# Gate projections as seven half-size products in a hybrid decoder layer on one core

## The chip, the cores and the metric

One core of one Trainium2 chip runs the whole program. The metric is device time in microseconds from launch to end. Before the change, three runs took 2067.43, 2071.05 and 2077.85 us, median 2071.05. A further execution was recorded by the hardware profiler; it took 2070.41 us, and its page and trace are what is read here.

## The reference

One layer of a decoder, 4096 tokens of width 1024, float32:

```python
h = _rmsnorm(x, g_pre) * (1.0 + scale[:, None]) + shift[:, None]
proj = h @ w_in
aq, ak, av, ag, rkv, rg, gq, gkk, gv, gg = jnp.split(proj, ...)
attn = _sliding_window_attention(...) * jax.nn.silu(ag)
rwkv = _rwkv7_mixer(h, ...) * jax.nn.silu(rg)
gla = _gla_mixer(h, gq, gkk, gv, ...) * jax.nn.silu(gg)
y = jnp.concatenate([attn, rwkv, gla], axis=-1) @ w_out
return x + gate[:, None] * _rmsnorm(y, g_post)
```

The gates `ag` (512 columns), `rg` and `gg` (256 each) are together one product of h (4096 x 1024) with a 1024 x 1024 weight. The change is about this product. The output product `@ w_out` has the same size.

## The kernel before

**Numbers.** Each float32 operand of a projection is split into a float16 high part and a float16 rest, and a product is three matmuls, high x high, high x rest and rest x high, added up in PSUM. Weights are scaled by a power of two before the split; the scale comes from the sum of their squares.

**Two phases.** Tokens go in 16 tiles of 256 (`NS = 16`, `NT = 256`). Phase one makes h of each tile (`stage_a`, kept in `hscr` as two float16 parts), and runs RWKV and GLA, whose results go to `mscr`. Beside it, `stage_c` prepares weights for phase two in small pieces: it reads a piece (tile `cs`), squares and sums it on ScalarE, splits it (ScalarE and VectorE, tile `ch`) and writes it to `wscr` (seven sets of 256 columns: two of q, one of k and v, four of gates) or, for the output product, to `woscr`. Phase two, from about 1000 us on, does per tile: q, k, v projections (`qkv`, `heads_of`; PSUM tiles `qp`, `kp`, `vp`), the gates (`gates`, `gates_of`; PSUM tile `gp`), the sliding-window attention (`stage_s`, `attend`; scores `sc`, values `ovp`), the mixing of heads and gates (`stage_m`), and the output product with its norm (`outp`, `norm`; PSUM tile `op`).

**The gates before.** `gates_of` makes four quarters of 256 channels. Each is 2 x 8 x 3 matmuls with weights as the stationary operand and 256 tokens of h as the moving one; ScalarE's tanh and one VectorE instruction per quarter make z (1 + tanh) of the PSUM bank in `ag`. All four weight quarters stay in SBUF. There are two `ag` buffers, used in turn.

**The output product** already has the form that the gates get: seven products of half size (Strassen's scheme in Winograd's form), whose weight sums are made in phase one (`wo_group`) and whose activation sums are made by VectorE in `stage_m`. Four of the seven weight sets stay in SBUF, three are streamed from `woscr` into one buffer `Wv`, half a set (512 KB) at a time. The activation blocks are split into `mtp`, four buffers in turn (`block`), scaled by `msc`; `msc` comes from the squares of the mixed tile, which a matmul with ones adds up over partitions (PSUM tile `mp`, then `mtot` and the small steps of `pow2` on VectorE). So the first block of a tile waits for all its gates.

**What sets the order.** The program is written as generators (`streams`, `emit`), and in each phase every instruction goes through `Order.note`, which gives it a rank: its place in the program, less `URGENT` for instructions that are marked urgent (PSUM drains). `Order.pin` then plays the program through with a table of costs and fixes the order of each engine's queue, lowest rank first among what is ready. The queues are worked in that order. The table of costs knows nothing of waits between VectorE and GpSimd. PSUM has two banks for projections and products (`pj`), so a product can start only when the one before the last has been drained.

In phase two, `stage_p2(i)` writes for most tiles: `gates(i)` after `outp(i - 1)`, then `qkv(i + 1)`. All instructions are issued through one helper line, so the profile shows them under L334 and they are told apart by their tiles.

## Time and profile before

| what | value |
|---|---|
| median of three runs | 2071.05 us |
| the profiled execution | 2070.41 us |
| its span, first to last instruction | 2068.6 us |
| mean granted TensorE clock | 0.986 |
| busy: TensorE, VectorE, ScalarE, GpSimd | 94%, 78%, 56%, 10% of the span |
| moved by DMA | 241.99 MB, mean 117 GB/s |
| chain that ended last, by engine | PE 57%, DVE 24%, DMA 8%, ACT 6% |

The span leaves 1.8 us of the execution outside it. PE is TensorE's matmuls, PEld its weight loads, DVE VectorE, ACT ScalarE, POOL GpSimd, SP the queue that issues DMAs. Matmuls are pipelined: one of 256 columns is listed with 273 ns but the next starts about 109 ns after it, so rates are read from start times. Neighbouring VectorE instructions overlap by some 0.08 us in the listing. In a group's row, the numbers behind the bar are busy time and mean ns of one instruction, then the idle time before them and what ended it.

### The profile page before, as it was taken

Reading aid. Unit: us, or ns where it says so; the run is one execution under the profiler, and the core shown is the slowest. Engines: PE = TensorE matmul, PEld = TensorE weight load, DVE = VectorE, ACT = ScalarE, POOL = GpSimd, SP = SyncE. Lnnn points to the kernel's source line nnn. Section 1 sums busy time; section 2 is a strip of 40 time slices with the busy share of each in tenths; the row PEclk is TensorE's granted clock in tenths of the full one; section 3 lists DMA queues with packets and bytes.
Section 4 is the critical chain, followed back from the end, with each engine's and each line's share of the span. In section 5 each row is a group of like instructions: output and inputs, shape, how many; then the busy total and the mean of one; then the engine's idle time right before and its main releaser. Section 6 shows DMA issues by size and latency. Waiting matters only on the chain.

```text
span 2068.6 us, 61564 instructions
## 1 busy us (share of the span) xinstructions
PE 1954.1 (94%) x24931; PEld 1516.6 (73%) x24931; DVE 1610.2 (78%) x5211; ACT 1154.7 (56%) x2765; POOL 216.6 (10%) x405
## 2 busy tenths in 40 slices
PE   5899999999999999999888999999999999999997
PEld 2677777787877877777667677777877777877783
DVE  5777878878777788987767878877778877778877
ACT  5867676677766856766334444453444444444543
POOL 0510111421111111111100000000000000000000
PEclk8999999999999999999999999999999999999999
DMA  9332232334222412446314534333334333334314
GB/s 344 126 95 80 74 97 72 108 104 120 81 93 68 138 45 92 119 122 177 117 43 151 166 113 146 105 134 107 123 116 142 109 126 115 114 125 128 123 45 175
DMA packets 183898, 241.99 MB, mean 117 GB/s; under 512 B 52195, under 2 KB 141748, under 8 KB 179382
## 3 DMA queue, kind: packets, MB, share of 16 engines
q1 hardware_dynamic: 183462, 237.45, 35.5%
q8 instruction: 198, 3.24, 0.7%
q14 instruction: 94, 0.77, 0.1%
q10 hardware_dynamic: 144, 0.52, 0.1%
HBM read 177.08 MB, written 60.82 MB: 115 GB/s over the span
## 4 chain that ended last, share of the span: by engine, by line
PE 57%; DVE 24%; DMA 8%; ACT 6%; issue 3%; SPq 2%; DVEq 0%; POOL 0%; ACTq 0%; POOLq 0%
PE gp L334 16%; PE op L334 12%; PE zz L334 5%; PE qp L334 3%; PE lp L334 3%; PE sc L334 2%; SPq L334 2%; DVE mtp L334 2%; DVE q L334 2%; PE ovp L334 2%; PE kp L334 2%; DVE pr L334 2%; PE pv L334 2%; DMA cs<-in_wo 1%; DMA cs<-in_w 1%
## 5 line engine op out<-in xcount | busy, mean ns | idle before, releaser
L334 PEld LDWEIGHTS <-mtp 128*128 128x128 f16 x1344 | 130.3, 98 | 140.9 <-issue 3.5
L334 PE MATMUL op<-o,mtp 128*128 128x512 f16 x768 | 172.3, 379 | 0.1
L334 ACT ACTIVATE pr<-pr,nm,lsc 128x256 f32<-128x256 f32 (+1 forms) x256 | 149.3, 585 | 33.7 <-DVE nm L334 33.7
L334 PE MATMUL op<-ov,mtp 128*128 128x512 f16 x576 | 143.1, 379 | 0.3 <-DVE q L334 0.2
L334 PEld LDWEIGHTS <-hT 128*128 128x128 f16 x1536 | 117.1, 99 | 25.8 <-DVE kg L334 4.3
L334 DVE CUSTOM_DVE_ANT_0 pr<-sc,ab,sinks 128x256 f32<-128x256 f32 (+1 forms) x256 | 108.6, 476 | 11.4 <-PE sc L334 11.1
L334 DVE TENSOR_TENSOR yv<-op,yv 128x512 f32<-128x512 f32 x105 | 70.4, 681 | 47.8 <-PE op L334 33.7
L334 PE MATMUL pv<-gvh,hT 128*128 128x272 f16 x512 | 100.1, 286 | 6.2 <-DVE kg L334 3.1
L334 ACT ACTIVATE ag<-gp,gh 128x512 f32<-128x512 f32 x64 | 43.7, 683 | 109.4 <-PE gp L334 109.4
L334 POOL COPY kT<-kT 128x512 f16<-128x512 f16 x15 | 10.2, 677 | 845.2 <-DVE kT L334 816.0
L334 ACT ACTIVATE mtp<-yv,oi 128x1024 f16<-128x1024 f32 x30 | 34.3, 1143 | 111.7 <-DVE yv L334 111.2
L334 PE MATMUL lp<-hT,Lh 128*128 128x256 f16 x512 | 92.4, 274 | 0.1
L334 PE MATMUL zz<-hT,rh 128*128 128x256 f16 x512 | 90.4, 276 | 0.0
L334 PE MATMUL zz<-hT,vh 128*128 128x256 f16 x512 | 88.8, 273 | 1.4 <-DVE zb L334 1.4
L334 DVE SCALAR_TENSOR_TENSOR ag<-ag,gp 128x512 f32<-128x512 f32 x64 | 43.8, 684 | 59.6 <-ACT ag L334 59.5
L334 PE MATMUL zz<-hT,kh 128*128 128x256 f16 x512 | 89.8, 273 | 0.0
L334 PE MATMUL gqk<-hT,gqkh 128*128 128x256 f16 x512 | 89.4, 275 | 0.0
L334 PE MATMUL gp<-hT,q3h 128*128 128x256 f16 x512 | 86.9, 274 | 1.9 <-DVE yv L334 1.4
L334 PE MATMUL gp<-hT,q5h 128*128 128x256 f16 x512 | 87.0, 273 | 1.4 <-DVE ag L334 1.4
L334 PE MATMUL qp<-hT,q1h 128*128 128x256 f16 x512 | 85.8, 273 | 0.6 <-DVE kT L334 0.6
L334 PE MATMUL qp<-hT,q0h 128*128 128x256 f16 x512 | 85.2, 273 | 1.1 <-DVE nwt L334 1.1
L334 PE MATMUL gp<-hT,q6h 128*128 128x256 f16 x512 | 85.5, 273 | 0.0
(460 smaller groups left out, 6046.0 us busy)
## 6 DMA issues: line engine op xcount, KB each, us to landing
ov<-woscr SPq DMA_DIRECT2D x96, 512.0 KB, 3.9
xt<-in_x SPq DMA_DIRECT2D x16, 1024.0 KB, 5.3
hscr<-hT SPq DMA_DIRECT2D x16, 1024.0 KB, 5.3
hT<-hscr SPq DMA_DIRECT2D x16, 1024.0 KB, 5.1
x<-in_x SPq DMA_DIRECT2D x30, 512.0 KB, 4.3
out<-yv SPq DMA_DIRECT2D x30, 512.0 KB, 2.9
cs<-in_w SPq DMA_DIRECT2D x112, 128.0 KB, 2.4
v<-vscr SPq DMA_DIRECT2D x128, 64.0 KB, 2.5
```

The source lines that it names most:

```text
L334: r = f(*args, **kw)
```

## The change

Seven products of half size replace the gates' eight half-size quarters of work (two halves of the channels x two halves of the contraction x two halves of the tokens):

- Weights. Phase one makes the seven weight sums of the gates (`group` with `gate` set, pieces of 512 columns) and keeps them in `gwscr`; the output product's sums go through the same function, in 8 groups instead of 16. `wscr` keeps only the three sets of q, k and v. The two column halves of the gates can have different scales, so the right half is first brought to the left half's (`g_r`).
- Activations. `sums`, per tile, makes four sums of quarters of h on GpSimd: four additions that join the high part and the rest, four additions and differences, and for each of the four sums a ScalarE copy to float16 and a GpSimd difference for the rest: 12 GpSimd instructions on 512 columns. Scratch tiles X, Y, Z are `xg`, the results `sg`.
- Products. `gates_of` runs seven products with a 128-column moving operand. ScalarE copies products 0 and 4 to X, VectorE adds the others to what is there already, GpSimd does two additions more (`g12`, and `Z`), and `close` makes z (1 + tanh) from SBUF with X, Y, Z as scratch.
- Streaming. Four of the gates' sets stay, three are streamed into `Wv`, which the output product uses too; `feed` issues the next half in the order in which the two products come (`runs`). The last tiles get buffers of their own (`ENDS`).
- Order. k and v are projected ahead of the gates and q after them (`mid`); the sums of the next tile are written behind q. One `ag` buffer is left. `URGENT` is 600 instead of 150, and block splits and `mix_scale` are marked urgent too.

```diff
-URGENT = 150
+URGENT = 600
...
+        def group(gate, k, c):
+
+            src, base, sc = (w2, 3, g_sc[c]) if gate else (wo, 0, wo_sc)
+            left, right = [wt([P, 512], "cs", 2).rearrange("p (h n) -> p h n", h=2) for _ in range(2)]
...
-            if 4 <= i < 6:
-                yield from wo_squares(i - 4)
-            elif 6 <= i < NS - 2:
-                for g in (i - 6, i + 2):
-                    yield from wo_group(g % 4, g // 4)
+            if 3 <= i < 5:
+                for n in (i, i + 2):
+                    yield from gate_squares(n)
+            elif 5 <= i < 7:
+                yield from wo_squares(i - 5)
+            for _ in range((0, 0, 0, 0, 1, 1, 1, 2, 2, 2, 2, 2, 2, 1, 0, 0)[i]):
+                yield from group(*next(groups))
...
+    PRODUCTS = ((0, False), (1, True), (6, True), (3, False), (4, True), (5, True), (2, False))
+    GATES = ((0, False), (6, True), (1, True), (4, False), (3, True), (5, True), (2, False))
...
+        def whole(t, i, j):
+            G.tensor_tensor(t, quarter(hT, 0, i, j), quarter(hT, 1, i, j), op=ALU.add)
+
+        def parts(t, n):
+            S.copy(to[n][:, 0], t)
+            G.tensor_tensor(to[n][:, 1], t, to[n][:, 0], op=ALU.subtract)
+
+        whole(X, 1, 0)
+        whole(Y, 1, 1)
+        G.tensor_tensor(Y, X, Y, op=ALU.add)
+        parts(Y, 0)
+        whole(Z, 0, 0)
+        G.tensor_tensor(Y, Y, Z, op=ALU.subtract)
+        parts(Y, 1)
+        G.tensor_tensor(X, Z, X, op=ALU.subtract)
+        parts(X, 2)
+        whole(Z, 0, 1)
+        G.tensor_tensor(Z, Z, Y, op=ALU.subtract)
+        parts(Z, 3)
...
-        for n in range(4):
-            yield ["pj"]
-            gp_ = pj("gp")
-            for b in range(2):
-                yield from proj(gp_[:, b * NT : (b + 1) * NT], Wq[3 + n], b * P, P, hT)
-            av = ag[:, 2 * n : 2 * n + 2, :].rearrange("p b n -> p (b n)")
-            model.order.urgent = URGENT
-            S.activation(av, gp_, AF.Tanh, scale=g_h[n])
-            V.scalar_tensor_tensor(av, av, 1.0, gp_, op0=ALU.add, op1=ALU.mult)
-            model.order.urgent = 0
+        moving = (a11, s2, a12, s3, s1, a22, s4)
+
+        def product(po, n):
+            w, stays = GATES[n]
...
+            for c in range(4):
+                for k in range(KD // 2):
+                    for a, b in ((0, 0), (0, 1), (1, 0)):
+                        PE.matmul(po[:, c], W[c // 2][:, c % 2, k, a, :], moving[n][b][:, k, :],
+                                  start=k == a == b == 0, stop=k == KD // 2 - 1 and a == 1)
...
+        def close(to, j, z, t):
+            for m in range(2):
+                S.activation(t[:, 2 * m : 2 * m + 2], z[:, 2 * m : 2 * m + 2], AF.Tanh, scale=g_h[2 * j + m])
+            V.scalar_tensor_tensor(to, t, 1.0, z, op0=ALU.add, op1=ALU.mult)
...
+        yield from full(4)
+        soon(S.copy, X, banks[4])
+        G.tensor_tensor(g12, g12, X, op=ALU.add)
+        G.tensor_tensor(Z, g22, X, op=ALU.add)
+        yield from full(5)
+        soon(V.tensor_tensor, g21, banks[5], g22, op=ALU.add)
+        close(g22, 1, Z, X)
+        close(g21, 0, g21, Y)
+        yield from full(6)
+        soon(V.tensor_tensor, g12, banks[6], g12, op=ALU.add)
+        close(g12, 1, g12, Z)
...
-        if 1 < i < NS - 1:
-            yield from gates(i)
-        load_h(i + 2)
-        if i + 1 < NS and "q" not in F[i + 1]:
-            yield from qkv(i + 1)
...
+        elif 1 < i < NS - 1:
+            if i < NS - 2:
+                yield from outp(i - 1)
+            yield from qkv(i + 1, gates(i))
...
+            load_h(i + 2)
+            yield from stage_u(i + 1)
```

What the change moves in the queues shows at three places of one steady tile. In the rows, a number behind a name tells buffers apart: `xg_18481`, `xg_18482` and `xg_18483` are X, Y and Z, and `sg_18476` to `sg_18479` the four sums.

On GpSimd in phase two, before: behind the last work of phase one, the halo copies of `kT` for 14 tiles stand in a row, and then the last tile's end.

```order
L334 COPY tf_543<-tc_17951 32x8x32 x4
L334 TENSOR_TENSOR ATm<-AT,tmask 32x256 x4
L334 MEMSET AS 128x16
L334 COPY tf_544<-tc_18571 32x8x32 x4
L334 COPY kT<-kT 128x4x128 x14
L334 TENSOR_TENSOR pr<-pr,xo_31975 128x512 x2
```

On GpSimd in a steady tile now: the last of the gates' two additions, then the sums of the next tile.

```order
L334 TENSOR_TENSOR xg_18483<-ag,xg_18481 128x512
L334 TENSOR_TENSOR xg_18481<-hT 128x512
L334 TENSOR_TENSOR xg_18482<-hT 128x512
L334 COPY kT<-kT 128x4x128
L334 TENSOR_TENSOR xg_18482<-xg_18481,xg_18482 128x512
L334 TENSOR_TENSOR xg_18483<-hT 128x512
L334 TENSOR_TENSOR sg_18476<-xg_18482,sg_18476 128x512
L334 TENSOR_TENSOR xg_18482<-xg_18482,xg_18483 128x512
L334 TENSOR_TENSOR xg_18481<-xg_18483,xg_18481 128x512
L334 TENSOR_TENSOR sg_18477<-xg_18482,sg_18477 128x512
L334 TENSOR_TENSOR sg_18478<-xg_18481,sg_18478 128x512
L334 TENSOR_TENSOR xg_18483<-hT 128x512
```

What moved: 14 additions a tile stand around the one copy. The first on `xg_18481` waits for the closing product that read X, the one on `xg_18483` for the closing product that read Z.

On VectorE before, from the last gates of a tile to the mixing: gatings of the mixed heads (`mxa`, `mxb`) stand between the gate products, with k's splits behind them.

```order
L334 TENSOR_TENSOR yv<-yv,x_19788 128x1024
L334 SCALAR_TENSOR_TENSOR mxa<-mxa,gh_106,ag 128x512
L334 SCALAR_TENSOR_TENSOR ag<-ag,gp 128x512
L334 SCALAR_TENSOR_TENSOR mxb<-mxb,gh_107,ag 128x512
L334 SCALAR_TENSOR_TENSOR ag<-ag,gp 128x512
L334 SCALAR_TENSOR_TENSOR mxb<-mxb,gh_108,ag 128x512
L334 TENSOR_TENSOR sm_27959<-mxa,mxb 128x512
L334 TENSOR_TENSOR mxa<-mxa 128x4x128
L334 SCALAR_TENSOR_TENSOR kT<-kp,kq_s,kT 64x256 x4
```

On VectorE now, the same stretch:

```order
L334 SCALAR_TENSOR_TENSOR ag<-xg_18481,xg_18483 128x4x128
L334 SCALAR_TENSOR_TENSOR ag<-xg_18482,ag 128x4x128
L334 SCALAR_TENSOR_TENSOR kT<-kp,kq_s,kT 64x256 x2
L334 TENSOR_TENSOR ag<-gp,ag 128x4x128
L334 SCALAR_TENSOR_TENSOR mxa<-mxa,gh_106,ag 128x512
L334 SCALAR_TENSOR_TENSOR mxa<-mxa,gh_107,ag 128x512
L334 SCALAR_TENSOR_TENSOR ag<-xg_18483,ag 128x4x128
L334 SCALAR_TENSOR_TENSOR mxb<-mxb,gh_108,ag 128x512
L334 SCALAR_TENSOR_TENSOR mxb<-mxb,gh_109,ag 128x512
L334 TENSOR_TENSOR sm_30617<-mxa,mxb 128x512
L334 TENSOR_TENSOR mxa<-mxa 128x4x128
L334 SCALAR_TENSOR_TENSOR q<-qp,q 64x512
```

What moved: all four gatings now stand behind the last PSUM addition, k's splits ahead of it, and the three closing products release X, Y and Z to GpSimd within this stretch.

On ScalarE before, from the last gates to the first block splits (`mtp<-mxa,msc`):

```order
L334 ACTIVATE ag_19796<-gp,gh_108 128x512
L334 ACTIVATE mtp,mss<-mxb 128x1024
L334 ACTIVATE kT<-kp,kq_s 64x256 x4
L334 ACTIVATE q<-qp 64x512 x2
L334 ACTIVATE mtp<-mxa,msc 128x512
```

On ScalarE now:

```order
L334 ACTIVATE mtp,mss<-mxa 128x1024
L334 CAST sg_18476<-xg_18482 128x512
L334 ACTIVATE mtp,mss<-mxb 128x1024
L334 ACTIVATE q<-qp 64x512
L334 CAST sg_18477<-xg_18482 128x512
L334 ACTIVATE q<-qp 64x512
L334 CAST sg_18478<-xg_18481 128x512
L334 ACTIVATE mtp<-mxa,msc 128x512
```

What moved: three casts, each of which waits for a GpSimd sum, stand ahead of the first block split; the square of the second half (`mtp,mss<-mxb`) stands behind the first of them.

More of the change, by code (lines that the diff above doesn't have):

```diff
@@ L1674, in heads_of @@
         model.order.urgent = 0
+        yield ["pj"]
+        vp = pj("vp")
+        for a in range(2):
+            yield from proj_tok(vp[:, a * P : (a + 1) * P], Wq[2], P, P, hT, a * P)
+        model.order.urgent = URGENT
+        S.activation(vt_.rearrange("p a n -> p (a n)"), vp[:, :NT], AF.Identity, scale=Wq[2][2])
+        model.order.urgent = 0
+        spread()
         for n in range(2):
-            yield ["pj"]
-            qp = pj("qp")
+            if n == 0 and mid is not None:
+                yield from mid
+            yield ["m" if n and pv is mq else "pj"]
+            qp = mt("qp") if n and pv is mq else pj("qp")
             for b in range(2):
@@ L1702, in gates, with stage_u @@
+    def stage_u(i):
+        load_h(i)
+        yield [F[i]["hT"]]
+        F[i]["S"] = blocks if i == 0 else sums_t
+        sums(F[i]["hT"], F[i]["S"])
     def gates(i):
-        yield [("og", i - 2)]
+        yield [("og", i - 1)] if i > 1 else []
         f = F[i]
-        f["ag"] = ag = t_A([P, 8, NT], "ag") if i == 0 else pools["ag"].tile([P, 8, NT], F32, name="ag2") if i == 1 else F[i - 2]["ag"]
-        yield from gates_of(f["hT"], ag, pjt)
+        f["ag"] = t_A([P, 8, NT], "ag") if i < 2 else F[1]["ag"]
+        yield from gates_of(f["hT"], f["S"], f["ag"], feed, own=Wx.get(("g", i)))
@@ L1850, in stage_m @@
         yield [mss, "mq"]
+        model.order.urgent = URGENT
         msc, f["oi"] = mix_scale(mss)
+        model.order.urgent = 0
         f["msc"] = msc
@@ L2047, in hybrid_kernel @@
     xo, gn = x2[:, 0, :], x2[:, 1, :]
-    mtp = pools["mtp"].tile([P, 4, 2, 4, P], F16, name="mtp")
-    blocks, split = [mtp[:, n] for n in range(4)], []
     streams((0, "v", stage_v, None), *((1, "s", stage_s, i) for i in range(1, NS)), *((2, "m", stage_m, i) for i in range(NS)),
@@ L2113, in hybrid_kernel, with load_g @@
                               mixf.rearrange("p b n -> p (b n)"))
+        for n, pair in zip((2, 0, 1), spare):
+            load_2(n, *pair)
+            Wq[n] = (*pair, w_inv[n])
+        def load_g(n):
+            SP.dma_start(Wv, gwscr[n])
         G.memset(fkT, 0.0)
```

292 lines of the change are left out of this document (185 added, 107 removed).

## Prediction, made before the run

> **What bounds the kernel now.** I read the page first, then the busy time by stage (PE, PEld, DVE, ACT, POOL, then granted clock, DMA share and GB/s).
>
> ```profile
> span 2068.6 us, 61564 instructions
> PE 1954.1 (94%) x24931; PEld 1516.6 (73%) x24931; DVE 1610.2 (78%) x5211; ACT 1154.7 (56%) x2765; POOL 216.6 (10%) x405
> ...
> 0.00:1000.00 1000.00, 930.41 (x13885) 743.12 (x13886) 786.65 (x2866) 680.11 (x1569) 196.64 (x374) 0.98 0.37 115
> 1000.00:1100.00 100.00, 89.01 (x1433) 70.27 (x1431) 65.44 (x256) 39.63 (x97) 8.53 (x16) 0.98 0.26 78
> ...
> 1400.00:1600.00 200.00, 197.36 (x2099) 151.78 (x2097) 154.64 (x426) 87.60 (x222) 1.84 (x3) 1.00 0.36 119
> ```
>
> From 1100 us on the second phase repeats one tile of 256 tokens. TensorE is busy 197.36 of 200 us there at clock 1.00, VectorE 154.64, GpSimd almost never. The timeline gives one tile's length, the rate of its matmuls, and its one TensorE wait.
>
> ```profile
> 1612.58 0.22 PE L334 MATMUL vp<-q2h,hT 128*128 128x128 f16 x1
> ...
> 1615.20 0.22 PE L334 MATMUL vp<-q2h,hT 128*128 128x128 f16 x1
> ...
> 1639.38 0.38 PE L334 MATMUL gp<-hT,q3h 128*128 128x256 f16 x2
> ...
> 1644.62 0.38 PE L334 MATMUL gp<-hT,q4h 128*128 128x256 f16 x2
> ...
> 1661.81 0.38 PE L334 MATMUL kp<-hT,q2h 128*128 128x256 f16 x2
> ...
> 1671.31 0.28 PE L334 MATMUL mp<-mss,ones 128*128 128x2 f32 x2
> ...
> 1678.60 1.89 PE L334 MATMUL op<-ov,mtp 128*128 128x512 f16 x8
> 1681.37 0.60 PE L334 MATMUL sc<-kT,q 128*128 128x256 f16 x4 [0.88 <-DVE m L334]
> ...
> 1701.86 0.38 PE L334 MATMUL gp<-hT,q3h 128*128 128x256 f16 x2
> ```
>
> A tile takes 1701.86 - 1639.38 = 62.48 us, of which TensorE waits 0.88 us. So in this phase every microsecond that TensorE is given less to do counts, until another chain takes its place.
>
> **TensorE's part.** One gate quarter was 48 matmuls over 256 columns in 1644.62 - 1639.38 = 5.24 us, 109.2 ns each; the four take 192 x 109.2 = 20.97 us a tile. The new form is 7 products x 4 column blocks x 4 k-blocks x 3 half-precision terms = 336 matmuls over 128 columns. That shape exists: the 48 `vp` matmuls, each with its own weight load, start 55.7 ns apart (2.62 us over 47). 336 x 55.7 = 18.72 us. Gain 2.25 us a tile, 36 us over 16 tiles if nothing else moves; the floor of a tile is then 62.48 - 2.25 = 60.23 us. The Trainium skill (TensorE: Matmul & The Clock Gate, section Back-to-back issue gap) speaks against this: it puts a sustained stream of weight load and matmul at about 81 ns for 128 columns, by which the seven products would take 27.2 us, more than the four quarters do now. The `vp` rows, the same pairs at the same width, say 55.7 ns, and I take the row.
>
> **VectorE, ScalarE and GpSimd.** Groups of one shape from 1200 to 1800 us (busy, mean ns), and GpSimd's and VectorE's durations in the first phase (minimum/median/maximum):
>
> ```profile
> L334 DVE TENSOR_TENSOR yv<-op,yv 128x512 f32<-128x512 f32 x64 | 42.9, 681 | 30.8 <-PE op L334 20.4 <-issue 10.5
> L334 DVE SCALAR_TENSOR_TENSOR ag<-ag,gp 128x512 f32<-128x512 f32 x40 | 27.4, 685 | 42.1 <-ACT ag L334 42.1
> L334 DVE SCALAR_TENSOR_TENSOR mxb<-mxb,gh,ag 128x512 f32<-128x512 f32 x20 | 15.0, 752 | 0.7
> ...
> L334 ACT ACTIVATE pr<-pr,nm,lsc 128x256 f32<-128x256 f32 x152 | 89.1, 588 | 18.8 <-DVE nm L334 18.8
> L334 ACT ACTIVATE ag<-gp,gh 128x512 f32<-128x512 f32 x40 | 27.3, 682 | 66.7 <-PE gp L334 66.7
> L334 ACT ACTIVATE mtp<-mxa,msc 128x512 f16<-128x512 f32 x28 | 20.1, 718 | 55.0 <-PE op L334 34.9 <-DVE msc L334 20.1
> L334 ACT COPY yv<-op 128x512 f32<-128x512 f32 x9 | 5.1, 567 | 0.0
> ...
> L334 POOL TENSOR_TENSOR gaw<-gaw,scol x16: 1034/1040/1566, 51.0 to 419.0; 128x512 f32<-128x512 f32 x16
> ...
> L334 DVE TENSOR_TENSOR KB<-ta,em x16: 678/686/1526, 89.3 to 1015.6; 128x512 f32<-128x512 f32 x16
> ...
> L334 DVE TENSOR_TENSOR AT<-atp,rmask x64: 674/682/693, 100.2 to 1024.6; 128x512 f32<-128x512 f32 x64
> ...
> L334 POOL COPY kT<-kT 128x512 f16<-128x512 f16 x15 | 10.2, 677 | 845.2 <-DVE kT L334 816.0 <-PE sc L334 29.2
> ```
>
> VectorE loses four gate products (685 ns) and gains four closing products from SBUF (752 ns) and five PSUM additions (681 ns): +3.7 us. Its 154.64 / 200 x 62.48 = 48.3 us become 52.0 of 60.2. ScalarE loses four 682 ns tanh and gains eight of half the width (at most 588 ns), two copies (567) and four casts (718 at most): +6.0 us on 27.4, no bound. GpSimd gets 14 additions of 1.04 us, 14.6 us a tile where it now does one copy. Its own time fits; what it costs VectorE is the question. Two engines side by side in the first phase:
>
> ```profile
> 389.95 1.18 POOL L334 TENSOR_TENSOR gaw<-gaw 128x256 f32<-128x256 f32 x1
> 391.10 1.49 POOL L334 TENSOR_TENSOR gaw<-gaw,scol 128x512 f32<-128x512 f32 x1
> ...
> 390.47 1.21 DVE L334 TENSOR_TENSOR RA<-zb,ep 128x512 f32<-128x512 f32 x1
> 391.61 1.52 DVE L334 TENSOR_TENSOR KB<-ta,em 128x512 f32<-128x512 f32 x1
> ```
>
> `KB` takes 0.69 us at the median and 1.52 here, and ends 0.54 us after GpSimd's `gaw` (391.61 + 1.52 against 391.10 + 1.49), as if it had been let in only near that one's end; `RA` before it lost 0.5 us the same way. So one 512-column GpSimd addition can cost a VectorE instruction that reads two SBUF tiles up to 0.84 us, and they take turns. An instruction with one input in PSUM does not wait: `AT<-atp,rmask` never took over 0.70 us in the same phase. Price of one of the 14: 0 to 0.84 us. The halo copy of `kT` (0.68 us) now stands third in GpSimd's queue behind two of the sums, some 8 us ahead of the scores that read it: nothing.
>
> **Where that price falls.** The gates of a tile end what its mixing waits for, and its first output product needs the first block:
>
> ```profile
> 1672.56 0.16 DVE L334 TENSOR_REDUCE mtot<-mp 128x1 f32<-128x2 f32 x1
> ...
> 1674.57 0.75 DVE L334 SCALAR_TENSOR_TENSOR mtp<-mxa,msc,mtp 128x512 f16<-128x512 f32 x1 [0.53 <-ACT mtp L334]
> ...
> 1664.24 1.06 ACT L334 ACTIVATE mtp<-mxb 128x1024 f16<-128x1024 f32 x1 [1.54 <-DVE mxb L334]
> ```
>
> Now the last gate matmul is followed by k, q, v and scores, 1678.60 - 1661.81 = 16.8 us of cover, and the block is there at 1675.32: 3.3 us to spare. The change moves k and v (24 x 109.2 and 48 x 55.7 ns, 5.3 us) ahead of the last gate products. Cover: 11.5 us. The chain in it, in the order of VectorE's queue: last PSUM addition 0.68, two gatings 1.50, the closing product 0.75, two gatings 1.50, ScalarE's square 1.06 and `mp` 0.28, one q split 0.69, then `mtot` to block 2.76 as now (1672.56 to 1675.32), and about 0.9 of hops: 10.1 us, 1.4 to spare. But GpSimd's next sums start as soon as the closing products have released its three scratch tiles, which is within this chain: nine or ten additions in a row, against seven VectorE instructions that read two SBUF tiles and stand ahead of `mtot` (four gatings, one closing product, the sum and the difference of the mixing). I take half of them hit, 3.5 x 0.84 = 2.9 us: 13.0 us of chain, 1.5 over the cover, a tile of 60.23 + 1.5 = 61.73. Queued behind: ScalarE's cast of a sum stands ahead of the first block's split, so a late GpSimd holds that too; that is inside the half that I take. Of the two `ag` buffers one is left; the first gate product of a tile comes 1701.86 - 1678.60 = 23 us after the mixing of the tile before was read: nothing. The larger priority number puts PSUM drains and block splits further ahead in the queues and adds no work.
>
> **The rest.** The streamed gate sets add 3 x 1 MB a tile to 72.92 MB in 600 us:
>
> ```profile
> DMA packets 29588, 72.92 MB, mean 122 GB/s; under 512 B 3152, under 2 KB 14672, under 8 KB 28240
> ...
> ov<-woscr SPq DMA_DIRECT2D x56, 512.0 KB, 3.9
> ```
>
> 7.6 MB a tile become 10.7; SyncE issues six more DMAs. A half set is asked for half a product before it is free altogether and needed two resident products later: 1.3 + 2 x 2.67 = 6.7 us, landing 3.9. I cost it at nothing; if landings pass 6.7 us the cover is gone. In the first phase the weight sums replace part of the splits:
>
> ```profile
> 0.00:1000.00 1000.00, 59.74 (x120) 103.21 (x312) 0.98 0.37 115
> ```
>
> That row is VectorE and ScalarE on the weight pieces. New: VectorE 16 x (0.48 + 3 x 0.75) + 12 x 0.75 = 53 us, and subtractions of double width, some 14 us more than now; ScalarE 48 squares and 76 splits, about 92 us. +7 and -11 us beside 930 us of TensorE work: 0, between -11 and +7. The gates of tiles 0 and 1 lie near 1000 to 1100 us, where TensorE has 11 us idle anyway: 0 to -4.5, taken as 0. Tile 15 has no sums beside its gates: -2.2.
>
> **Sum.** The profiled execution took 2070.4 us (span 2068.6 and 1.8 around it; the median of the runs, 2071.05, is the same within 0.03%). Thirteen steady tiles x (62.48 - 61.73) = 9.8, tile 15 2.2: 2070.4 - 12.0 = 2058.4, say 2058.
>
> **Rivals.** (1) GpSimd stays clear of the chain. For it: 1.4 us to spare, and GpSimd and VectorE also run undisturbed (the medians above). Then every tile is 60.23: 14 x 2.25 = 31.5, and up to 4.5 from tiles 0 and 1: 2034 to 2039. (2) Slower: strict turns, as at 391 us, on the whole chain. All seven hit, 5.9 us: chain 16.0, 4.5 over the cover, a tile of 64.7: 13 x 2.25 = 29 more, less 2.2: 2097. It decides between gain and loss from (1.4 + 2.25) / 0.84 = 4.3 hits of seven on. For it: VectorE would be at 52.0 + 5.9 of 64.7 us, so there is little slack to catch up in. This is the Trainium skill's rule (SBUF — State Buffer, section Who interferes with whom: a VectorE instruction with two SBUF inputs and a GpSimd one that reads SBUF exclude each other for a whole instruction); the rows at 391 us agree, the medians show how often it bites. (3) Streams late: landings of 9 us would hold two products a tile for 2.3 us each: 60.2 + 4.6, 2070 + 30 = 2100. Nothing in DMA's 36% share speaks for it. (4) The weight loads bound the narrow matmuls: one is listed with 99 ns, and if a pair could not start faster, 336 x 0.099 = 33.3 us, 12.3 a tile more, 2267.
>
> ```profile
> L334 PEld LDWEIGHTS <-hT 128*128 128x128 f16 x1536 | 117.1, 99 | 25.8 <-DVE kg L334 4.3
> ```
>
> The `vp` rows speak against it, and 73% busy PEld overlaps PE.
>
> **Chances.** Forecast 0.40 (two to five hits: 2043 to 2075), rival 1 0.27, rival 2 0.23, rival 3 0.07, rival 4 0.03. The range runs from rival 1 to rival 2, 2034 to 2098, and leaves out rivals 3 and 4. About 0.5% is what a measurement of this kernel can tell from no change (2060 to 2081): faster is rival 1 and half of the forecast, 0.47; same is the other half and 0.04 of rival 2's lower side, 0.24; slower is the rest, 0.29.
>
> **What would show it.** Right: `gp` matmuls 56 ns apart; GpSimd near 25% in phase two; gatings and closing products with maxima of 1.5 us; TensorE waiting 1 to 3 us a tile before the first `op`, put down to `mtp`; a tile of 61 to 63 us. Wrong: no wait there (rival 1); a wait over 4 us, or waits on `ovp` and `sc` behind a late VectorE (rival 2); `ov` named as a releaser (rival 3); gate matmuls more than 80 ns apart (rival 4); or a first phase that ends more than 10 us earlier or later.

## The result and the profile after

| | before | after |
|---|---|---|
| median of 4 runs, us | 2070.33 (2067.43 to 2077.85) | 2199.3 (2195.26 to 2210.12) |
| the profiled execution, us (its span) | 2070.41 (2068.6) | 2210.12 (2208.3) |
| start of the first tile's `mp`, us | 1122.5 | 1129.0 |
| one steady tile, us | 62.48 | 72.36 |
| from the 14th `mp` to the end, us | 147.4 | 160.2 |

The ratio is 1.0625, 95% interval 1.0577 to 1.0674: 6% slower, where 0.6% faster was forecast and 2098 was the end of the range. A steady tile is here, and in all that follows, the mean distance of the `mp` matmuls (one pair a tile) between the 4th and the 13th tile. Of the 139.7 us between the profiled spans, 6.5 are there at the first `mp`, 120.5 come in the 13 tiles to the 14th `mp` (9.3 a tile), 12.8 at the end.

The page of after, its busy time by stage (PE, PEld, DVE, ACT, POOL, then granted clock, DMA share, GB/s):

```profile
span 2208.3 us, 66379 instructions
PE 1988.6 (90%) x27235; PEld 1552.8 (70%) x27235; DVE 1782.6 (81%) x5265; ACT 1218.8 (55%) x2785; POOL 538.0 (24%) x629
...
0.00:1000.00 1000.00, 931.73 (x13810) 745.25 (x13810) 810.89 (x2831) 672.04 (x1439) 217.43 (x385) 0.97 0.36 113
...
1200.00:2000.00 800.00, 704.64 (x8614) 537.11 (x8613) 648.95 (x1541) 362.33 (x892) 233.02 (x165) 0.94 0.44 148
```

The first phase is as it was. In the steady phase TensorE is busy 704.64 of 800 us, where the same stretch of before has

```profile
1200.00:2000.00 800.00, 788.93 (x8312) 605.87 (x8297) 626.19 (x1747) 359.24 (x918) 7.36 (x12) 1.00 0.36 120
```

and its clock is 0.94 instead of 1.00. Per tile that is 788.93 / 800 x 62.48 = 61.6 us busy and 0.9 waiting before, 704.64 / 800 x 72.36 = 63.7 busy and 8.6 waiting after. The change takes 2.25 us of matmuls out of a tile, so busy should be 59.4: 63.7 - 59.4 = 4.3 us are longer busy time, most of it matmuls that run slower, 8.6 - 0.9 = 7.7 are new waits, and -2.25 + 4.3 + 7.7 is, within rounding, the tile's loss of 9.9. (Some 0.7 of the 4.3 us, by an estimate, are only the listing: the last matmul before a wait stands there with its whole 273 ns instead of the 109 to the next one, and a tile has about five waits instead of one.) What the waits of TensorE after 1100 us are for (us, times, longest):

```profile
PE mp L334 <- ACT mtp L334: 43.3, 12, 4.5
PE sc L334 <- DVE m L334: 28.0, 28, 1.7
PE gp L334 <- DMA ov<-gwscr: 21.4, 12, 3.5
PE op L334 <- ACT yv L334: 13.4, 9, 3.7
PE ovp L334 <- DVE pr L334: 6.3, 4, 2.3
```

The largest stands between the last gates and the first block, but before `mp`, where the prediction expected it before the first `op`. One such place: TensorE, then VectorE, then GpSimd, from the first `qp` behind the last gate matmul on (start, duration).

```profile
1601.05 0.38 PE L334 MATMUL qp<-hT,q0h 128*128 128x256 f16 x2
...
1607.60 0.27 PE L334 MATMUL qp<-hT,q1h 128*128 128x256 f16 x1
1611.41 0.38 PE L334 MATMUL mp<-mss,ones 128*128 128x2 f32 x2 [3.54 <-ACT mtp L334]
1611.65 0.27 PE L334 MATMUL qp<-hT,q1h 128*128 128x256 f16 x1
...
1612.74 0.63 PE L334 MATMUL qp<-hT,q1h 128*128 128x256 f16 x2
1613.16 0.42 PE L334 MATMUL qp<-hT,q1l 128*128 128x256 f16 x1
...
1618.01 0.84 PE L334 MATMUL op<-ov,mtp 128*128 128x512 f16 x3
```

```profile
1602.52 0.69 DVE L334 TENSOR_TENSOR ag<-gp,ag 128x512 f32<-128x512 f32 x1
1603.13 2.02 DVE L334 SCALAR_TENSOR_TENSOR mxa<-mxa,gh,ag 128x512 f32<-128x512 f32 x2
1605.08 1.76 DVE L334 SCALAR_TENSOR_TENSOR ag<-xg,ag 128x512 f32<-128x512 f32 x1
1606.87 3.30 DVE L334 SCALAR_TENSOR_TENSOR mxb<-mxb,gh,ag 128x512 f32<-128x512 f32 x2
1610.21 1.64 DVE L334 TENSOR_TENSOR sm<-mxa,mxb 128x512 f32<-128x512 f32 x1
1611.95 1.57 DVE L334 TENSOR_TENSOR mxa<-mxa 128x512 f32<-128x512 f32 x1
...
1614.27 0.16 DVE L334 TENSOR_REDUCE mtot<-mp 128x1 f32<-128x2 f32 x1
...
1616.68 1.73 DVE L334 SCALAR_TENSOR_TENSOR mtp<-mxa,msc,mtp 128x512 f16<-128x512 f32 x1
```

```profile
1604.57 1.72 POOL L334 TENSOR_TENSOR xg<-xg,xg 128x512 f32<-128x512 f32 x1
1606.92 1.15 POOL L334 TENSOR_TENSOR xg<-hT 128x512 f32<-128x512 f16 x1 [0.63 <-DVE ag L334]
1608.03 1.60 POOL L334 TENSOR_TENSOR sg<-xg,sg 128x512 f16<-128x512 f32 x1
1609.70 3.27 POOL L334 TENSOR_TENSOR xg<-xg,xg 128x512 f32<-128x512 f32 x2
```

VectorE and GpSimd go one after the other. The closing product takes 1.76 us (0.68 undisturbed), the `mxb` gatings 1.65 each (0.75), the sum and difference of the mixing 1.64 and 1.57 (0.69); most of GpSimd's additions 1.6 (1.15 where they are not held). The seven VectorE instructions that the prediction listed take 2.02 + 1.76 + 3.30 + 1.64 + 1.57 = 10.3 us where 2 x 0.75 + 0.68 + 2 x 0.75 + 2 x 0.69 = 5.1 stand undisturbed. It is so in every tile from the fourth to the 14th: each of the seven takes the same time within 0.02 us, and `mp` waits 3.53 or 3.54 us. After that wait TensorE's `qp` matmuls, 0.11 us apart until 1612, go 0.21 us apart up to about 1615.7: the 35 behind `mp` take 5.65 us instead of 4.0.

### The profile page after: what moved, and what is told of

The parts are those of the page before. It is cut to its first block, busy times and chain, and to the rows that moved or that the text cites. A ratio compares the mean times of both kernels' runs of the same rounds, so it can differ in the third digit from the quotient of the medians.

```text
span 2208.3 us, 66379 instructions
## 1 busy us (share of the span) xinstructions
PE 1988.6 (90%) x27235; PEld 1552.8 (70%) x27235; DVE 1782.6 (81%) x5265; ACT 1218.8 (55%) x2785; POOL 538.0 (24%) x629
## 3 DMA queue, kind: packets, MB, share of 16 engines
q8 instruction: 216, 3.54, 0.7%
## 4 chain that ended last, share of the span: by engine, by line
PE 45%; DVE 35%; DMA 9%; issue 4%; ACT 4%; SPq 3%; POOL 0%; DVEq 0%; ACTq 0%; POOLq 0%
PE op L334 8%; PE gp L334 7%; PE zz L334 7%; DVE pr L334 4%; DVE mtp L334 3%; DVE ag L334 3%; SPq L334 3%; DMA ov<-gwscr 3%; PE lp L334 3%; PE kp L334 2%; PE gqk L334 2%; DVE mxb L334 2%; PE pv L334 2%; DVE mxa L334 2%; DVE q L334 2%
## 5 line engine op out<-in xcount | busy, mean ns | idle before, releaser
L334 PEld LDWEIGHTS <-g 128*128 128x128 f16 x3072 | 176.6, 98 | 4.9 <-issue 3.5
L334 PEld LDWEIGHTS <-ov 128*128 128x128 f16 x2256 | 135.4, 100 | 25.5 <-DMA ov<-gwscr 23.6
L334 PE MATMUL gp<-sg,ov 128*128 128x128 f16 x1440 | 93.0, 226 | 21.4 <-DMA ov<-gwscr 21.4
L334 POOL TENSOR_TENSOR sg<-xg,sg 128x512 f16<-128x512 f32 x60 | 83.5, 1395 | 94.3 <-ACT sg L334 67.3
L334 PE MATMUL sc<-kT,q 128*128 128x256 f16 (+1 forms) x512 | 78.5, 285 | 29.3 <-DVE m L334 28.0
L334 POOL TENSOR_TENSOR xg<-xg,xg 128x512 f32<-128x512 f32 x64 | 99.5, 1562 | 2.7
L334 POOL TENSOR_TENSOR xg<-hT 128x512 f32<-128x512 f16 x64 | 78.5, 1237 | 84.9 <-ACT xg L334 60.9
L334 PE MATMUL gp<-hT,g 128*128 128x128 f16 x1536 | 96.4, 220 | 1.1 <-ACT xg L334 1.1
L334 PEld LDWEIGHTS <-q 128*128 128x128 f16 x512 | 49.7, 101 | 66.9 <-issue 52.3
L334 DVE TENSOR_TENSOR ag<-gp,ag 128x512 f32<-128x512 f32 x48 | 32.9, 686 | 78.7 <-PE gp L334 78.3
```

The source lines that it names most:

```text
L334: r = f(*args, **kw)
```

## The experiments

Eighteen kernels ran, each beside the kernel before on the same chip (its median there 2069.5 to 2070.9). "Busy" and "waiting" are TensorE's in a steady tile, worked out as above from the stretch 1200 to 2000 us. x1, x5, x6, x9 and x18 leave out work that the layer needs.

| kernel | us | ratio to before, 95% | tile | busy | waiting |
|---|---|---|---|---|---|
| before | 2070 | | 62.5 | 61.6 | 0.9 |
| after | 2199.3 | 1.0625 (1.0577 to 1.0674) | 72.4 | 63.7 | 8.6 |
| x1 sums once | 2083.9 | 1.0069 (1.0050 to 1.0088) | 63.2 | 60.4 | 2.9 |
| x5 small gate stream | 2161.5 | 1.0457 (1.0415 to 1.0499) | 68.5 | 62.3 | 6.2 |
| x6 = x1 + x5 | 2068.2 | 0.9998 (0.9981 to 1.0016) | 61.6 | 60.0 | 1.6 |
| x18 = x6 + k, v behind | 2061.8 | 0.9945 (0.9929 to 0.9961) | 60.7 | 59.4 | 1.4 |
| x10 k, v behind | 2164.1 | 1.0455 (1.0420 to 1.0490) | 68.2 | 62.2 | 6.0 |
| x4 late sums | 2120.0 | 1.0240 (1.0211 to 1.0269) | 65.0 | 60.7 | 4.4 |
| x9 = x4 + x5 | 2109.3 | 1.0191 (1.0160 to 1.0222) | 64.5 | 60.6 | 3.9 |
| x8 = x4, other sets stay | 2128.8 | 1.0275 (1.0231 to 1.0320) | 65.0 | 60.5 | 4.5 |
| x11 = x4 + x10 | 2098.8 | 1.0143 (1.0115 to 1.0170) | 62.9 | 59.7 | 3.2 |
| x13 = x11, old tail | 2097.3 | 1.0128 (1.0109 to 1.0146) | 62.8 | 60.1 | 2.7 |
| x2 sums on VectorE | 2145.0 | 1.0356 (1.0309 to 1.0404) | 67.1 | 62.4 | 4.7 |
| x7 = x2, late | 2122.5 | 1.0254 (1.0220 to 1.0289) | 65.3 | 61.3 | 4.0 |
| x17 = x7 + x10 | 2128.4 | 1.0292 (1.0264 to 1.0321) | 65.7 | 61.3 | 4.4 |
| x3 casts on GpSimd | 2222.4 | 1.0735 (1.0705 to 1.0765) | 73.1 | 63.5 | 9.7 |
| x12 URGENT 150 | 2219.1 | 1.0709 (1.0681 to 1.0737) | 74.6 | 64.6 | 10.0 |
| x14 before + unread sums | 2130.6 | 1.0289 (1.0266 to 1.0312) | 67.0 | 62.9 | 4.1 |
| x15 = x14, late | 2142.7 | 1.0352 (1.0327 to 1.0376) | 68.2 | 63.8 | 4.4 |
| x16 before, URGENT 600 | 2070.6 | 1.0005 (0.9991 to 1.0019) | 62.5 | | |

A set of sums is twelve additions on GpSimd, two more belong to the gates; the expectations up to x13 say ten by mistake, and 6.9 us for them on VectorE where it is 12 x 0.69 = 8.3.

**x1: the sums for two tiles only.**

```
-        sums(F[i]["hT"], F[i]["S"])
+        if i < 2:
+            sums(F[i]["hT"], F[i]["S"])
```

> The activation sums are made for tiles 0 and 1 only; later tiles multiply with stale sums, so this kernel leaves out 10 GpSimd additions and 4 ScalarE casts a tile. Theory A (GpSimd's sums and VectorE's instructions with two SBUF inputs take turns, and everything else that is late follows from that): the steady tile falls from 71.6 us to 60.2 to 61.5, TensorE's waits for mtp and m nearly go, its clock comes back to 1.00, time 2199 - 13 x 10.5 = 2045 to 2075. Theory B (the new order of the work is late by itself: shorter cover behind the last gate product, the streams of gate weights, ScalarE's longer queue): the tile stays over 66 us, time over 2125.

The time falls by 115 us, most of the loss, and the wait for `mtp` before `mp` is gone; what stands in its place (1100 us to the end):

```profile
PE gp L334 <- DMA ov<-gwscr: 19.8, 11, 3.1
PE sc L334 <- DVE m L334: 15.6, 27, 0.8
```

So Theory A has the main cause, but not the whole: 63.2 us is 3 over the floor, between the two theories, and with the sums left out from tile 2 on the kernel is still slower than before.

**x5: the gate sets streamed for 16 of 128 partitions** (`cut` is true for gate sets from tile 2 on). **x6: that and x1.**

```
-            SP.dma_start(Wv[:, 2 * h : 2 * h + 2], src[n, :, 2 * h : 2 * h + 2])
+            rows = slice(0, 16) if cut else slice(0, P)
+            SP.dma_start(Wv[rows, 2 * h : 2 * h + 2], src[n, rows, 2 * h : 2 * h + 2])
```

> From tile 2 on the streamed gate sets are loaded for 16 of their 128 partitions only (the other rows stay stale), so 7/8 of the 3 MB a tile of gate weights are left out; the order of DMAs is kept. Theory A (the streams are a follow-up of late TensorE work, not a cause): TensorE's 21 us of waits for ov<-gwscr go at most, time 2175 to 2200. Theory E (the streams hold TensorE, x and the output DMAs too): tile under 67 us, time under 2140.

> Both at once: the sums for tiles 0 and 1 only, and the streamed gate sets for 16 of 128 partitions from tile 2 on; both parts are left out. Theory F (two causes, the sums and the streams, and nothing else): what is left is the seven products, tile 60.3 to 61.5 us, time 2035 to 2055, so under the kernel before. Theory G (a third cost, in the order of the work or ScalarE): the tile stays over 62 us and the time over 2065.

The streams cost 72.4 - 68.5 = 3.9 us a tile beside the sums and 63.2 - 61.6 = 1.6 without them, between the two theories for x5. In x6 the tile is nearly Theory F's, the time Theory G's: 61.6 us a tile, and no gain. Why a stream is late is seen on SyncE's queue of after:

```profile
1717.55 0.37 SPq L334 DMA_DIRECT2D vscr<-vt  x1
1721.15 3.64 SPq L334 DMA_DIRECT2D v<-vscr  x8
1724.89 1.67 SPq L334 DMA_DIRECT2D ov<-gwscr  x2
1726.66 0.38 SPq L334 DMA_DIRECT2D out<-yv  x1
1727.09 0.42 SPq L334 DMA_DIRECT2D x<-in_x  x1
```

The first gate product, which streams its set, began at 1718.8 us. The request for the next set stands behind the eight loads of v, which wait for v's own round trip through memory, and goes out at 1724.9; 1 MB of other transfers follows it at once. Its first half lands after 4.65 us, its second, beside those transfers, after 7.27. TensorE then stands before the fourth gate product:

```profile
1729.59 1.51 PE L334 MATMUL gp<-sg,ov 128*128 128x128 f16 x24 [1.66 <-DMA ov<-gwscr]
...
1732.68 0.51 PE L334 MATMUL gp<-sg,ov 128*128 128x128 f16 x6 [1.30 <-DMA ov<-gwscr]
```

In 11 of the 12 waits of after for `ov<-gwscr` the late request stands right behind the loads of v.

**x10: k and v back behind the gates. x18: that with the sums and streams out.**

```
-            yield from qkv(i + 1, gates(i))
+            if 3 <= i < NS - 3:
+                yield from gates(i)
+                yield from qkv(i + 1)
+            else:
+                yield from qkv(i + 1, gates(i))
```

> For tiles 3 to 12 the k and v products go back behind the last gate product, as in the kernel before; the cover of the chain from the last gate product to the first block is then about 5.3 us longer; nothing is left out. Theory A (the turns lengthen the chain, and also all of VectorE's other work): the waits for mtp go (3.6 us in a tile) and the clock rises, tile 66 to 69 us, time 2125 to 2170. Theory H (the shorter cover alone is the loss): tile under 64 us, time under 2115. Theory V (VectorE bounds the tile anyway): tile over 70 us, time over 2180.

> Sums for tiles 0 and 1 only, streamed gate sets for 16 of 128 partitions, and k and v behind the gates for tiles 3 to 12: the sums of the other tiles and 7/8 of the streams are left out. All three suspected costs are gone, so the tile shows what the seven products save: 60.2 to 60.8 us by the prediction's 2.25 us, time 2052 to 2062. A tile over 61.5 us would say that the saving itself is smaller.

x10's time is Theory A's, its waits are not: the wait before `mp` did not go (1200 to 1900 us).

```profile
PE mp L334 <- DVE kT L334: 43.8, 9, 5.2
PE sc L334 <- DVE m L334: 9.4, 10, 1.3
PE gp L334 <- DMA ov<-gwscr: 4.4, 6, 1.3
```

`mp` now comes behind k, v and 23 of the `qp`, and is put down to `kT`: k and `mp` share a bank of PSUM (`mq`), and VectorE's drains of k stand behind the slow gatings. In the tile at 1524 us the square is done at 1521.1, the last `kT` at 1524.2, and `mp` runs at 1524.4. So x10 does not show the cover by itself; some of its 4.2 us a tile comes from the third row (with v behind the gates its loads are no longer ahead of the streams; 17.7 us in the same stretch of after became 4.4) and from fewer waits for `m`. x18 settles the products: 60.7 us a tile, 59.4 of them busy, which is before's 61.6 less 2.25, at clock 1.00 in all four quarters of the steady phase; as time the tile is 1.75 us shorter, since it waits 0.5 us longer. It is 0.55% faster than before, without most of the work that the seven products need.

**x4: the sums held until the fourth block is split. x9: with small streams. x8: with other sets kept** (the second diff). **x11: with k and v behind.**

```
         F[i]["S"] = blocks if i == 0 else sums_t
+        if 2 < i < NS - 1:
+            yield [("m", i - 1)]
+            for t in xg:
+                V.tensor_copy(t[:, 0, 0:1], F[i - 1]["blk"][3][:, 1, 0, 0:1])
```

```
-    GATES = ((0, False), (6, True), (1, True), (4, False), (3, True), (5, True), (2, False))
+    GATES = ((0, True), (6, False), (1, True), (4, True), (3, False), (5, True), (2, False))
```

> From tile 3 on the sums wait for the split of the fourth block of the tile before, by three one-column copies into their scratch tiles; the same 10 additions and 4 casts, 20 to 25 us later, beside the softmax. Theory A (the turns matter only on the chain from the gates to the first block): tile 62 to 64 us, time 2075 to 2110, no TensorE wait over 1 us for mtp. Theory D (they cost VectorE the same wherever they lie, as VectorE is busy 80% of the time): the waits move to sc and ovp, tile 67 us or more, time over 2140.

> The late sums, and the streamed gate sets for 16 of 128 partitions only (7/8 of them left out). Theory E1 (landing times): as with the shifted sets, tile 64.0 to 64.6, 2105 to 2118. Theory E2 (the bytes cost beside the sums as they do in the kernel after, where the small streams gave 3.7 us a tile): tile 61 to 62.5, time 2060 to 2085.

> The late sums, and another choice of which gate sets stay: products 1, 3, 4 and 6 of the seven stay, 2, 5 and 7 are streamed, so that the streamed set behind the last output product has one more product of cover; nothing is left out. Theory E1 (the streams cost by their landing times at that one place): the last waits for ov go, tile 64.0 to 64.6 us against 65.0, time 2105 to 2118. Theory E2 (they cost by their bytes, beside other transfers): no change, 2115 to 2125.

> The late sums and k and v behind the gates together; nothing is left out. With the sums late the chain has no turn in it and TensorE waits for mp only 0.3 us a tile, so Theory A expects little: tile 64 to 65.2 us, time 2105 to 2125. Theory H (cover) expects it near the kernel before, tile 62.5 us or less, under 2085.

The same work, begun 15 us behind the last gate matmul instead of at once, gives back 7.3 of 9.9 us a tile. In x4 TensorE's waits are short (1300 to 1900 us), and its clock is 0.99 to 1.00:

```profile
PE sc L334 <- DVE m L334: 18.1, 22, 1.2
PE ovp L334 <- DVE pr L334: 8.2, 9, 1.0
PE vp L334 <- DVE yv L334: 5.4, 9, 0.7
PE gp L334 <- DMA ov<-gwscr: 3.3, 3, 1.8
PE mp L334 <- ACT mtp L334: 2.9, 5, 0.6
```

The result lies between Theories A and D: off the chain the turns cost less, but not nothing, and the waits move to the softmax, as D has it. Without the collisions on the chain the streams cost 0.5 us (x9, in Theory E1's range), and keeping other sets gains nothing (x8, against Theory E1). x11 comes to 62.9 us a tile, half a microsecond over before, with nothing left out; Theory A was too pessimistic by 1.1 us, H too hopeful.

**x13: x11 to the last tile, and the last output products in the old order.**

```
-            if i < NS - 2:
-                yield from outp(i - 1)
+            yield from outp(i - 1)
...
-            if i == NS - 2:
-                yield from outp(i - 1)
```

> The late sums with k and v behind the gates, now for tiles 3 to 14, and the tail in the order of the kernel before (the output products of tile 13 ahead of the gates of tile 14); nothing is left out. Theory A and the tail: the steady tile stays 62.7 us, so level with the kernel before; the tail, 11 us longer so far, comes within 5 us: 2078 to 2092. If the seven products could gain once nothing collides, it comes under 2060.

The tile stays, the tail does not get shorter (163.8 us from the 14th `mp`, 158.5 in x11). That guess falls. The tail is not quite that of the kernel before: there q, k and v of the last tile stand ahead of the gates of tile 14, here behind them. In x1 and x6 the tail is 148.3 and 148.2 us beside 147.4 before, so most of after's 12.8 us there are the sums too. In x13 the steady tile is only 0.35 us over before's; of the 21.6 us between the profiled spans 16.4 are the tail.

**x2, x7, x17: the twelve additions on VectorE; early, late, and late with k and v behind.** One of the lines:

```
-            G.tensor_tensor(t, quarter(hT, 0, i, j), quarter(hT, 1, i, j), op=ALU.add)
+            V.tensor_tensor(t, quarter(hT, 0, i, j), quarter(hT, 1, i, j), op=ALU.add)
```

> The 10 additions of a tile stand on VectorE instead of GpSimd, nothing is left out. Theory A (turns): VectorE gets about 10 x 0.69 = 6.9 us more work of its own but loses the blocked time; 52 + 6.9 = 59 us of VectorE a tile beside 60.2 of TensorE, so a tile of 62 to 65 us, 2070 to 2115. Theory C (it is the mere amount of vector work in the chain from the gates to the first block, on whichever engine): the sums now stand in VectorE's own queue ahead of that chain, tile 68 us or more, time over 2150.

> The sums late as in the kernel with the late sums, and on VectorE; nothing is left out. Theory A (turns): 10 x 0.69 = 6.9 us of VectorE work a tile in place of 10 additions on GpSimd that take turns with it; VectorE 59 to 60 us a tile: 63 to 65 us a tile, 2085 to 2120, about the late sums on GpSimd. Theory C (amount): VectorE bounds the tile, 66 us or more, over 2135.

> Late sums on VectorE with k and v behind the gates for tiles 3 to 12; nothing is left out. No GpSimd instruction but the two additions of the gates and the halo copy is left to take turns with, and VectorE has 12 x 0.69 = 8.3 us more of its own. Theory C (amount): 52 + 8.3 = 60.3 us of VectorE a tile leave it no slack beside 60.2 of TensorE, tile 63.5 us or more, 2100 or more. Theory A (only turns cost): tile 61 to 62.5 us, 2075 to 2095.

65.3 to 67.1 us a tile. x2 is nearer to Theory C, x7 just over Theory A's range, x17 within Theory C's. On VectorE the sums meet few turns, yet each order is slower than before; late is better than early by 1.8 us (x7). VectorE is 86 to 88% busy in these kernels (78% before, 1200 to 2000 us). That this leaves it too little slack is not shown: the streams are late here as well, with 12 to 15 us of waits for `ov<-gwscr` in the 800.

**x3: the casts of the sums on GpSimd** (the diff). **x12: URGENT back at 150. x16: before with URGENT 600.**

```
-            S.copy(to[n][:, 0], t)
+            G.tensor_copy(to[n][:, 0], t)
```

> The four casts of a tile's sums go from ScalarE to GpSimd, so that no ScalarE instruction waits for GpSimd in the sums; GpSimd gets 4 copies of 1.07 us more; nothing is left out. Theory S (ScalarE's queue is held behind late sums, and with it the square ahead of mp and the first block): tile 69.5 us or less, time under 2175. Theory A (VectorE and GpSimd in turns is the loss, ScalarE is not held): no gain, rather 0 to 3 us a tile more, 2195 to 2240.

> URGENT is 150 again, all else as in the kernel after. Theory A: the number only orders what is ready at the same time; 2180 to 2215. Theory U (the number 600 lets splits and drains pass work that the chain needs): under 2160.

> The kernel before with URGENT 600, nothing else. In the kernel after, 150 in its place cost 20 us. Theory U (the larger number helps any order of this work): 2050 to 2062. Theory A (it helps only where VectorE is late): 2066 to 2075.

x3: 0.8 us a tile more, so ScalarE's casts are not what holds the chain; in after's piece, too, the square of `mxb` starts at 1610.21 us, right at the end of its gating. That the 0.8 us are four more turns is likely, not shown. The larger priority number is worth 20 us to the kernel after, more than either theory of x12 allowed, and nothing to the one before (x16); no run takes the reason apart.

**x14, x15: the kernel before, with one set of sums a tile that nobody reads.** The additions, casts and subtractions are those of `sums`, into three float tiles and a half-precision one; they start behind one-column copies from the last closing product (x14, the first line below, written behind `gates(i)`) or from the fourth block's split (x15, the second, behind `block(i, 3)`).

```
+            sums(F[i + 1]["hT"], F[i]["ag"][:, 7, 0:1])
+            sums(F[i + 1]["hT"], f["blk"][3][:, 1, 0, 0:1])
```

> The kernel before, and beside it the twelve GpSimd additions and four ScalarE casts of one set of sums per tile (twelve, not the ten that earlier expectations say), from tile 3 on, started by the last closing product of the tile before; nobody reads the results, TensorE's order is that of the kernel before. Theory A (turns): the same chain, with 3.3 us to spare here, gets 6 to 9 us longer: a tile of 65 to 68 us, 2100 to 2140, gatings and splits at 1.6 to 1.75 us. Theory B (the sums only hurt together with the new order and the shorter cover): 62.5 to 63 us a tile, 2068 to 2078.

> The same unread sums in the kernel before, started by the split of the fourth block instead. Theory A: the turns fall beside the softmax, off the chain: 62.5 to 64 us a tile, 2068 to 2092. Theory D (the sums cost wherever they lie): as with the early ones, 2100 or more.

This is the sums alone: no new gates, no streams, the old cover, in x14 TensorE's old order. They cost 67.0 - 62.5 = 4.5 us a tile, twice the 2.25 us of TensorE's work that the seven products save. x14's main wait of TensorE (1200 to 1900 us; the other is 0.7 us a tile before `qp`), three rows of its VectorE, and its `op` behind the wait:

```profile
PE sc L334 <- DVE m L334: 34.1, 10, 3.4
```

```profile
1505.35 1.65 DVE L334 TENSOR_TENSOR mxa<-sm,mxa 128x512 f32<-128x512 f32 x1
1506.92 1.64 DVE L334 SCALAR_TENSOR_TENSOR mtp<-mxb,msc,mtp 128x512 f16<-128x512 f32 x1
...
1512.62 0.48 DVE L334 CUSTOM_DVE_ANT_0 pr<-sc,ab,sinks 128x256 f32<-128x256 f32 x1
```

```profile
1513.57 0.60 PE L334 MATMUL sc<-kT,q 128*128 128x256 f16 x4 [3.41 <-DVE m L334]
...
1515.35 1.06 PE L334 MATMUL op<-ov,mtp 128*128 128x512 f16 x2
```

The longer cover takes the delay of `mp` here, and the delay comes out one step later: the score maxima (`pr<-sc,ab,sinks`) stand in VectorE's queue behind the slow splits, and the next scores wait 3.4 us for them, once in every tile. Late sums are no better in this kernel, so Theory D is right there. x15's VectorE beside them:

```profile
1518.25 1.22 DVE L334 TENSOR_TENSOR nm<-m,fneg 128x8 f32<-128x8 f32 x1
1519.39 0.15 DVE L334 TENSOR_TENSOR es<-sinks,m 128x8 f32<-128x8 f32 x1
1519.58 1.24 DVE L334 TENSOR_TENSOR es<-es,lsc 128x8 f32<-128x8 f32 x1
...
1526.52 1.09 DVE L334 TENSOR_SCALAR pr<-pr,rd 128x256 f32<-128x256 f32 x1
```

Instructions of eight columns (0.16 us undisturbed) wait for a whole addition of 512, and so do some scalings of the softmax (0.35). The delay also passes through ScalarE: its exponentials start late, behind `nm`, with casts of the sums between them, and VectorE stands still until ScalarE's `es` is there:

```profile
DVE sm L334 <- ACT es L334: 34.9, 11, 3.4
```

The next split stands in VectorE's queue behind all this, and `op` waits for `mtp` 3.1 us a tile.

## Why the prediction was wrong, point by point

**The products: right.** The matmuls of after start 55.8 ns apart (48 of `gp<-sg,g` between 1652.46 and 1655.14 us in this piece):

```profile
1652.46 2.84 PE L334 MATMUL gp<-sg,g 128*128 128x128 f16 x48
1655.14 1.06 PE L334 MATMUL gp<-hT,g 128*128 128x128 f16 x16
```

x18 shows the 2.25 us as busy time of TensorE, and 1.75 us of them as time. Rival 4 falls, and with it the 81 ns that the Trainium skill (TensorE: Matmul & The Clock Gate, section Back-to-back issue gap) gives.

**The step that failed: "I take half of them hit, 3.5 x 0.84 = 2.9 us".** All seven are hit, two by 0.3 us and five by 0.9 to 1.1, for 10.3 - 5.1 = 5.2 us together: rival 2's 5.9, almost, and its mechanism. By the prediction's own sum all seven give a tile of 64.7 us, so this step makes 3.0 of the 72.36 - 61.73 = 10.6 us by which the tile was missed. The chain from the last gate matmul to the first `op` takes 1618.01 - 1601.05 = 17.0 us. TensorE's work in it is the predicted cover of 11.5 us within half a microsecond (6.8 + 0.3 + 4.0 + 0.9); wait and slow matmuls make up the other 5. The median of the first phase was the wrong witness for how often it bites: there GpSimd is busy 196.64 of 1000 us, here it is a row of eleven additions and a copy from 1601 to 1619.5 us with gaps of 0.6 and 1.0, and each VectorE instruction meets the next of the row.

**The place of the wait.** The prediction set the whole chain, up to the first block, against the whole cover. But `mp` stands in TensorE's queue behind 61 of the 96 `qp` matmuls. So the part of the chain that ends with `mp` has 6.8 us of TensorE's work beside it, and the 35 `qp` behind `mp` (4.0 us) can only start after it. With the sums late (x4) the longest wait there is 0.6 us.

**The second: 1.04 us an addition.** Most of GpSimd's additions take 1.6 us in the row, since they wait as well. GpSimd is 24% busy over the whole span, but 233.02 of 800 us in the steady stretch: 21.1 us a tile with the copy, where the prediction had 14.6 us of additions and near 25%. Its row of sums reaches from 1601 to 1625 us, over the block splits, which the sum had as undisturbed (2.76 us from `mtot` to block; 4.14 in this tile, 1614.27 to 1618.41).

**What the sum lacked: the way on.** Rival 2 had the hits right and gave 64.7 us, 7.7 too little, because a delay was counted once, against one cover, and the streams at nothing (below). First, waits slow the matmuls after them: 4.3 us a tile of longer busy time, with the granted clock at 0.5 for 89 of the 800 us; most of it is gone where the waits are about 1 us (busy 60.7, 59.7 and 59.4 in x4, x11 and x18). Secondly, x14 shows that a longer cover passes the delay on to the next reader of VectorE. Such are the waits for `m` in after, which the prediction's list named only as a sign of rival 2; that the waits for `yv` come the same way is likely, not shown.

**The streams: not nothing.** Rival 3's sign was there (`ov` as releaser, 21.4 us), its mechanism in single cases only: the median landing rose from 3.9 to 4.6 us, within the 6.7 us counted (the page of after, us from issue to landing), and two of the 50 gate halves timed between 1200 and 2000 us took longer, 7.3 and 7.4.

```profile
ov<-gwscr SPq DMA_DIRECT2D x94, 512.0 KB, 4.6
```

The term failed because the window was counted from when a half is free, while SyncE sends requests in order, and v's eight loads, moved ahead by the same change, stand in front (x10, with v behind the gates, has 4.4 us of these waits where after has 17.7). The streams cost 1.6 us a tile alone, 3.9 beside the sums.

**The cover:** counted right as TensorE's work, 16.8 to 11.5 us. The old order of k and v is worth 0.9 us a tile without the sums (x6 against x18) and 4.2 with them (x10); neither is the cover alone, since `mp` and v's loads move too.

**Costed at nothing, and so it was:** the first phase (its last solver matmul starts at 1066.0 us, 1068.4 before), ScalarE in the chain of after (x3), the priority number in the kernel before (x16). Open: the first `mp` lies anywhere from 1118.7 to 1130.3 us in the variants, so that after's 6.5 us there cannot be put down to anything; and the step from the second to the third tile is 72.6 us in x6 and x18 where before has 66.5 and x4 66.4, which no run takes apart. With both, x18, whose tile is 1.75 us shorter, gains only 9 us in all.

No version of the seven products that leaves nothing out beats the kernel before; the nearest is x13, 1.3% slower. Two runs give the balance of a tile: the products save 2.25 us of TensorE's work and 1.75 us of time (x18), and their sums cost 4.5 us on GpSimd even under the longer cover of the kernel before (x14). With the sums late and k and v behind the gates (x11, x13) the steady tile is 0.35 to 0.5 us over before's.

## What to carry to other kernels

GpSimd is not a free engine beside a busy VectorE: price its work as if both engines did it, one instruction at a time, and as if every VectorE instruction with both inputs in SBUF were hit in that stretch. Place such work by what VectorE does next to it, not by whether its own engine is idle (x4 against after: 7.3 us a tile for the same work). Set a chain against the work that stands ahead of its own next instruction in TensorE's queue, here `mp`, not against all that follows. And count a delay on to its second and third reader, and the slow matmuls behind the wait, before calling it covered.

## What the runs showed of the hardware

- Steady turns: with both engines loaded, neither starves. VectorE's 0.69 us become 1.64, GpSimd's 1.15 become 1.60. This is the Trainium skill's rule (SBUF — State Buffer, section Who interferes with whom), and VectorE's instructions with both inputs in SBUF agree with it in the pieces above, while `ag<-gp,ag`, with one input in PSUM, keeps its 0.69 us beside an addition of GpSimd. What a turn costs is set by the other's instruction: 0.16 us became 1.22. In x15 `pr<-pr,rd`, with one tile and a value per row as inputs, was held too: 0.35 us became 1.09.
- Clock: between 1200 and 2000 us the trace of after has 19 stretches of 3.4 or 6.8 us at a granted clock of 0.5, all a whole number of 3.41 us apart. About 1 us after the wait of 3.54 us the `qp` matmuls went from 0.11 to 0.21 us, for some 3.3 us; that one wait cost 1.65 us more than itself. Not every such wait does it: eight of the eleven before `mp`, and seven of twelve waits of 3.4 us in x14, where `op` goes at 0.42 instead of 0.22 us. Seven other stretches of after follow two waits close together, of 1.34 and 1.73 us. In x4, where most waits are near 1 us, the clock stays at 0.99 to 1.00. The Trainium skill (TensorE: Matmul & The Clock Gate, section Part 1: The HAM clock gate) says as much: half rate until TensorE has been busy for some 3.4 us.
- One request queue: eight loads on SyncE, which waited for a round trip until 1721.15 us and then took 3.64 us to issue, held up a 1 MB stream whose buffer had been read by 1722.6 us, and TensorE 3 us.
